# A two-layer hybrid block in float32: the nets' activations made with tokens in rows and turned by DMA and VectorE

## The chip, the core and the metric

The kernel runs on one core of a Trainium2 chip. Its engines work at the same time, each through its own queue: TensorE multiplies (PE in the profile, with its weight loads as PEld), VectorE (DVE) and ScalarE (ACT) do the element-wise work, GpSimd (POOL) a little, and SyncE (SP) issues nearly all transfers. The metric is device time in microseconds (us) of one execution; lower is better. A time is the median of several runs, and the profile is of one execution.

## What is computed

256 tokens of width 1024 pass two layers (DEPTH = 2), each with four steps and a layer norm behind each:

```python
for l in range(DEPTH):
    h = layer_norm(ALPHA * h + 0.5 * swiglu(h, ffn1_gate[l], ffn1_up[l], ffn1_down[l]), ...)
    z = h @ w_in[l]        # split into a short gated convolution, a gated linear recurrence (hgrn2), a pool
    mix = jnp.concatenate([y_conv, y_rec, y_pool], axis=-1) @ w_out[l]
    h = layer_norm(ALPHA * h + mix, ...)
    h = layer_norm(ALPHA * h + cross_attn(h, mem, ca_q[l], ca_k[l], ca_v[l], ca_o[l]), ...)
    h = layer_norm(ALPHA * h + 0.5 * swiglu(h, ffn2_gate[l], ffn2_up[l], ffn2_down[l]), ...)

def swiglu(x, w_gate, w_up, w_down):
    return (jax.nn.silu(x @ w_gate) * (x @ w_up)) @ w_down
```

All of it is float32. The nets' hidden width D_FF is 2816; the attention has 4 heads of 256 over 256 memory tokens. The change touches the nets (`swiglu`, four in all), the first loads of the mixer, and the attention.

## The kernel before

**Precision.** TensorE's fast float32 format (F32R) keeps fewer bits, so every operand is kept as a high and a low part: `split` (lines 60 to 62) has ScalarE cast the high part and VectorE subtract it from the source for the low part. A product is then high x high, high x low and low x high, summed in PSUM. `load` (64 to 91) brings weights by SP in pieces of 1 MB into three buffers `raw`, and splits each piece into two tiles `whi` and two tiles `wlo` of 128 x 1024, of which there are eight each.

**Two forms of a product.** `mm_rows` (127 to 130) has tokens in the output's rows: the activations are the stationary operand, 512 columns of weights stream, three matmuls for each step of 128 in the depth. `mm_cols` (112 to 119) has output features in the rows: the weights are stationary, and the activations' high and low parts stream side by side (512 columns) behind the high weights, and the high part alone (256 columns) behind the low ones, two matmuls for each step; the two sums lie interleaved, and `add` (121 to 124) copies one by ScalarE and adds the other by VectorE. A 512-wide block of features over 256 tokens takes 48 matmuls in the first form and 64 in the second.

**The nets** (`ffn`, 364 to 533) go through the hidden width in chunks of 512, five of them and a last one of 256. For a chunk, gate and up give activations `silu(gate) * up`; `down` then needs them with hidden units in the partitions, as the tiles `ah` and `al` (three pairs). The first chunk (`first`, 374 to 453) is made with tokens in rows, since the weights can be used as they come; its activations are turned by TensorE, eight 128 x 128 transposes into PSUM (`turn`, 391 to 395, line 394), and split from there. The second half of these turnings is put behind the first products of the next chunk (`late`). All other chunks (`hidden`, 455 to 477) are made with hidden units in rows, so nothing is turned. The products with `down` of chunk c - 2's second half and of chunk c - 1's first half follow each chunk (`both`, 493 to 499), into four PSUM banks `dn` that hold the sums over all chunks; the last three slabs make the tail. Other products use four PSUM banks `acc`.

**The joints.** `finish` (284 to 330) adds the residual, takes the norm in steps on VectorE (statistics, then lines 322 and 326 on each half of the row), one token tile after the other. Tile 1's transposes are handed on as `pend` and are run in the middle of the next step's independent products: among the keys (`keys`) ahead of the mixer, among the values (`values`) ahead of the queries, inside the first chunk of a net. The mixer's first matrix (`columns(1280, ...)`) and the queries (`query`) use the normed activations `xT` right after.

**The attention** (815 to 897) makes queries, `weights` (scores and softmax of a head), values, then for each head `turned` (858 to 866: four transposes of the softmax by TensorE, line 862, and a split) and `mixed` (868 to 877: the product with the values). Heads 0 and 1 are turned among the values, heads 2 and 3 after the products of heads 0 and 1.

**What sets the order.** The framework's planner orders each engine's instructions when the program is built, from the order in which they are written, their dependencies and its own costs; each engine then runs its list in order. `tc.issue_after(x)` puts a block's instructions behind x on x's own engine; under `manual_schedule` the written order holds. SP's list holds the transfers: one that waits for its source or its buffer holds up those behind it.

Of the kernel before, what the change touches and what calls it, by code (L numbers as in the profile page):

```python
# [8 lines left out]
F32 = mybir.dt.float32  # L9
# [3 lines left out]
ALU = mybir.AluOpType  # L13
# [33 lines left out]
def model(ctx: ExitStack, tc: tile.TileContext, t: dict, out: bass.AP):  # L47
# [9 lines left out]

    loads = []

# [3 lines left out]

    def load(src, k0, nk, c0, ncol, fine=False):


        hi, lo, todo = [], [], []
        step = 2048 // ncol
        for a in range(k0, k0 + nk, step):
            raw = wp.tile([P, 2048], F32, tag="raw", name="raw", bufs=3)  # L70
            raw = raw.rearrange("p (k c) -> p k c", c=ncol)
            half = step // 2
            part = 1 if fine else step
            for b in range(0, step, part):
                loads.append(nc.sync.dma_start(
                    raw[:, b : b + part, :],
                    src[(a + b) * P : (a + b + part) * P, c0 : c0 + ncol].rearrange("(k p) c -> p k c", p=P),
                ))
# [12 lines left out]
        return Weights(hi, lo, half, todo)  # L91
# [40 lines left out]
    def tok(i):  # L132
        return slice(i * P, (i + 1) * P)
# [150 lines left out]
    def finish(mm, y, scale, gb, last=False, flip=False):  # L284
# [6 lines left out]
        for i in range(NT):  # L291
# [33 lines left out]
            for c in pieces:  # L325
                nc.vector.scalar_tensor_tensor(h[i][:, c], h[i][:, c], rs, b[:, c], op0=ALU.mult, op1=ALU.add)  # L326
# [37 lines left out]
    def ffn(l, name, n, pend=None, last=False, early=None):  # L364
        gate, up, down = (t[f"{name}_{x}"][l] for x in ("gate", "up", "down"))
        with tc.tile_pool(name="ffn", bufs=2, reuse_waits="tile") as fp:
            acts, marks = [], []

            def act_tiles():
                ah = fp.tile([P, 4, SEQ], F32R, tag="ah", name="ah", bufs=3)  # L370
                al = fp.tile([P, 4, SEQ], F32R, tag="al", name="al", bufs=3)
                return ah, al

            def first():

                ah, al = act_tiles()
# [3 lines left out]
                def products(o, w, i, k):  # L380
                    wh, wl = w.at(k, slice(0, CHUNK))
                    mm_rows(o, xTh[:, k, tok(i)], xTl[:, k, tok(i)], wh, wl, k == 0, k == NK - 1)

                def activate(og, ou):
                    s = fp.tile([P, CHUNK], F32, tag="sg", name="sg", bufs=3)
                    v = halves(s)
                    nc.scalar.activation(v, sums(og), AF.Silu)
                    marks.append(nc.vector.tensor_tensor(v, sums(ou), v, op=ALU.mult))
                    return s

                def turn(i, s):
                    pt = acc((P, 4, P))
                    for k in range(4):
                        nc.tensor.transpose(pt[:, k, :], s[:, k * P : (k + 1) * P], idn)  # L394
                    split(ah[:, :, tok(i)], al[:, :, tok(i)], pt)

                if pend is None:
# [34 lines left out]
                    wu = load(up, 0, NK, 0, CHUNK)  # L432
                    ou = [acc((P, CHUNK)) for _ in range(NT)]
                    for a in range(0, NK, 2):
                        for i in range(NT):
                            for k in range(a, a + 2):
                                products(ou[i], wu, i, k)
                    s = [activate(og[i], ou[i]) for i in range(NT)]
                else:
                    s = []  # L440
                    for i in range(NT):
                        og = acc((P, CHUNK))
                        for k in range(NK):
                            products(og, wg, i, k)
                        ou = acc((P, CHUNK))
# [4 lines left out]
                        s.append(activate(og, ou))  # L450
                if pend is not None:
                    turn(0, s[0])
                return (ah, al), lambda: [turn(i, s[i]) for i in range(NT) if i or pend is None]

            def hidden(c0, ncol, late):
                nt = ncol // P
                ah, al = act_tiles()
                w = load(gate, 0, NK, c0, ncol)
                sg = []
                for p in range(nt // 2):  # L460
                    s = fp.tile([P, 2, SEQ], F32, tag="sg", name="sg", bufs=3)
                    for j in range(2):
                        add(s[:, j, :], mm_cols(w, slice((2 * p + j) * P, (2 * p + j + 1) * P), xT))
                    nc.scalar.activation(s, s, AF.Silu)
                    sg.append(s)
                    if late is not None and p == 0:
                        late()
                with tc.issue_after(marks[-1].ins) if late is not None else nullcontext():
                    w = load(up, 0, NK, c0, ncol)
                for p in range(nt // 2):  # L470
                    s = sg[p]
                    r = fp.tile([P, 2, SEQ], F32, tag="up", name="up")
                    for j in range(2):
                        add(r[:, j, :], mm_cols(w, slice((2 * p + j) * P, (2 * p + j + 1) * P), xT))
                    nc.vector.tensor_tensor(s, r, s, op=ALU.mult)
                    split(ah[:, 2 * p : 2 * p + 2, :], al[:, 2 * p : 2 * p + 2, :], s)
                return ah, al

            def slab(c, u):
                w = load(down, c * 4 + 2 * u, 2, 0, DM)  # L480
                ah, al = acts[c]
                return w, ah[:, 2 * u : 2 * u + 2, :], al[:, 2 * u : 2 * u + 2, :]
# [17 lines left out]

            late = None
            for c, (c0, ncol) in enumerate(chunks):
                if c:
                    acts.append(hidden(c0, ncol, late))
                    late = None
                else:
                    a, late = first()
                    acts.append(a)
                    ys = [[acc((P, 512), "dn") for _ in range(2)] for _ in range(NT)]
                if c == 1:  # L510
# [50 lines left out]
    def mixer(l, fill):  # L561
        w_in = t["w_in"][l]
        with tc.tile_pool(name="mix", bufs=1, reuse_waits="tile") as mp:

            def columns(c0, ncol, take, behind=lambda p: None):
                w = load(w_in, 0, NK, c0, ncol)
# [25 lines left out]

            for _ in columns(1280, 512, lambda j, o: add(f[:, :, j, :], o), ev_f):
                pass
# [220 lines left out]
    def attention(l, pend):  # L815
        scale = (DM // HEADS) ** -0.5
        with tc.tile_pool(name="att", bufs=1, reuse_waits="tile") as ap:
# [6 lines left out]
            def query(c, between=None):  # L824
                w = load(t["ca_q"][l], 0, NK, c * CHUNK, CHUNK)
                for p in range(2):
# [31 lines left out]
            def turned(hh):  # L858
                pt = acc()
                for i in range(NT):  # L860
                    for m in range(NT):
                        nc.tensor.transpose(pt[:, m, tok(i)], pr[hh][:, i, tok(m)], idn)
                pTh = ap.tile([P, NT, SEQ], F32R, tag="pTh", name="pTh", bufs=2)
                pTl = ap.tile([P, NT, SEQ], F32R, tag="pTl", name="pTl", bufs=2)
                split(pTh, pTl, pt)
                return pTh, pTl

            def mixed(hh, pT):
# [69 lines left out]
```

## Time and profile before

| what | value |
|---|---|
| time, median of 3 runs (lowest to highest) | 1111.46 us (1111.36 to 1111.53) |
| the profiled execution's own time | 1111.42 us |
| its span (first to last instruction) | 1109.6 us |
| TensorE busy / its weight loads | 1098.6 / 989.2 us |
| VectorE / ScalarE / GpSimd busy | 819.1 / 605.4 / 62.5 us |
| granted TensorE clock | 0.998 |
| moved by DMA | 218.23 MB, mean 197 GB/s |

Busy time is the sum of an engine's instructions. Matmuls overlap in the profile, each being shown for longer than the distance to the next start: the pace is read from the distance of starts, or from a stretch of the chain divided by its count. In rows such as `start us, us, engine line op out<-in xN [idle <-releaser]` the bracket tells how long the engine was idle before and what released it.

### The profile page before, as it was taken

The numbers are of one execution on the slowest core, as the hardware profiler recorded it, in microseconds if no ns is written. First come the engines' busy times: TensorE is split into PE (matmuls) and PEld (weight loads), VectorE is DVE, ScalarE is ACT, GpSimd is POOL, SyncE is SP. The second block draws the span as 40 slices with busy tenths as digits, with TensorE's granted clock in tenths as the row PEclk, the third lists the DMA queues.
The fourth block names the chain that finished last, engine by engine and source line by source line (L and its number), as shares of the span: only waits on it lengthen the run. The fifth ranks groups of instructions, "written<-read, shape, count | busy, mean of one in ns | idle before, by whom it ended". The sixth has DMA issues, their size and how long they took to land.

```text
span 1109.6 us, 15784 instructions
## 1 busy us (share of the span) xinstructions
PE 1098.6 (99%) x6211; PEld 989.2 (89%) x6211; DVE 819.1 (74%) x1177; ACT 605.4 (55%) x895; POOL 62.5 (6%) x112
## 2 busy tenths in 40 slices
PE   9999999999999999999999999999999999999997
PEld 7999988999889889999889999889998998999896
DVE  6777668898888766566677666598988777666665
ACT  6566454665557365555455555456564654654550
POOL 9500000000000000000000000000000000000000
PEclk9999999999999999999999999999999999999999
DMA  8956655744475365665467555655535645656541
GB/s 318 299 185 228 227 199 176 244 142 152 167 268 172 106 236 202 216 228 192 150 229 256 199 192 186 228 190 190 173 133 203 213 154 181 234 190 215 178 177 38
DMA packets 99114, 218.23 MB, mean 197 GB/s; under 512 B 4256, under 2 KB 16832, under 8 KB 99040
## 3 DMA queue, kind: packets, MB, share of 16 engines
q1 hardware_dynamic: 97248, 214.84, 56.4%
q0 software_dynamic: 1216, 1.20, 0.4%
q10 hardware_dynamic: 576, 1.18, 0.3%
q8 instruction: 49, 0.80, 0.3%
q14 instruction: 25, 0.20, 0.1%
HBM read 216.15 MB, written 1.05 MB: 196 GB/s over the span
## 4 chain that ended last, share of the span: by engine, by line
PE 93%; DVE 5%; issue 1%; DMA 0%; ACT 0%; DVEq 0%
PE acc L103 61%; PE dn L103 28%; DVE wlo L62 2%; PE dn L687 1%; PE acc L167 1%; DVE h L326 1%; DVE xT L62 0%; DVE h L312 0%; DVE h L322 0%; PE dn L741 0%; PE dn L664 0%; DMA h<-in_x_dram 0%; PE acc L394 0%; DVE st L314 0%; DVE pTl L62 0%
## 5 line engine op out<-in xcount | busy, mean ns | idle before, releaser
L62 DVE TENSOR_TENSOR wlo<-raw,whi 128x1024 fp32r<-128x1024 f32 (+1 forms) x396 | 470.3, 1211 | 101.2 <-ACT whi L61 66.7
L61 ACT CAST whi<-raw 128x1024 fp32r<-128x1024 f32 (+1 forms) x396 | 398.1, 1041 | 170.8 <-PE dn L103 126.8
L103 PE MATMUL acc<-xT,whi 128*128 128x512 f32 x1600 | 388.3, 381 | 0.7 <-DVE xT L62 0.7
L103 PEld LDWEIGHTS acc<-xT,whi 128*128 128x128 f32 x1600 | 288.9, 190 | 33.8 <-DVE xT L62 1.1
L103 PEld LDWEIGHTS acc<-xT,wlo 128*128 128x128 f32 x1600 | 209.7, 191 | 10.7
L103 PE MATMUL acc<-xT,wlo 128*128 128x256 f32 x1600 | 210.8, 275 | 0.0
L103 PE MATMUL dn<-whi,ah 128*128 128x512 f32 x346 | 131.5, 380 | 0.0
L103 PE MATMUL dn<-wlo,ah 128*128 128x512 f32 x346 | 131.1, 379 | 0.0
L103 PE MATMUL dn<-whi,al 128*128 128x512 f32 x346 | 131.1, 379 | 0.0
L103 PE MATMUL acc<-whi,xT 128*128 128x512 f32 x288 | 88.4, 381 | 0.0
L103 PE MATMUL dn<-whi,xT 128*128 128x512 f32 x288 | 88.3, 382 | 0.1
L124 DVE TENSOR_TENSOR sg<-acc,sg 128x256 f32<-128x256 f32 x72 | 30.4, 422 | 67.4 <-ACT sg L123 67.3
L103 PEld LDWEIGHTS dn<-whi,al 128*128 128x128 f32 x346 | 65.4, 189 | 9.3
L103 PEld LDWEIGHTS dn<-wlo,ah 128*128 128x128 f32 x346 | 65.4, 189 | 9.2
L103 PEld LDWEIGHTS dn<-whi,ah 128*128 128x128 f32 x346 | 65.5, 189 | 8.7
L123 ACT COPY sg<-acc 128x256 f32<-128x256 f32 x72 | 26.7, 371 | 77.9 <-PE acc L103 77.9
L319 POOL TENSOR_TENSOR rs<-rs,nhalf 128x1 f32<-128x1 f32 x16 | 15.0, 934 | 873.7 <-DVE rs L318 873.7
L103 PEld LDWEIGHTS dn<-whi,xT 128*128 128x128 f32 x288 | 54.2, 189 | 7.9 <-ACT whi L61 0.5
L103 PEld LDWEIGHTS acc<-whi,xT 128*128 128x128 f32 x288 | 54.3, 189 | 7.6
L103 PE MATMUL dn<-wlo,xT 128*128 128x512 f32 x144 | 54.8, 380 | 0.3 <-DVE wlo L62 0.3
L103 PE MATMUL acc<-wlo,xT 128*128 128x512 f32 x144 | 54.6, 379 | 0.0
L123 ACT COPY up<-acc 128x256 f32<-128x256 f32 x72 | 26.6, 371 | 46.4 <-PE acc L103 45.3
(196 smaller groups left out, 1070.9 us busy)
## 6 DMA issues: line engine op xcount, KB each, us to landing
raw<-in_ffn_up_dram SPq DMA_DIRECT2D x44, 1024.0 KB, 5.0
raw<-in_ffn_down_dram SPq DMA_DIRECT2D x44, 1024.0 KB, 4.9
raw<-in_ffn_gate_dram SPq DMA_DIRECT2D x42, 1024.0 KB, 5.0
raw<-in_w_in_dram SPq DMA_DIRECT2D x24, 1024.0 KB, 5.0
raw<-in_ca_k_dram SPq DMA_DIRECT2D x8, 1024.0 KB, 4.9
raw<-in_w_out_dram SPq DMA_DIRECT2D x8, 1024.0 KB, 4.9
raw<-in_ca_v_dram SPq DMA_DIRECT2D x8, 1024.0 KB, 5.7
raw<-in_ca_q_dram SPq DMA_DIRECT2D x8, 1024.0 KB, 4.9
```

The source lines that it names most:

```text
L61: nc.scalar.copy(hi, src)
L62: nc.vector.tensor_tensor(lo, src, hi.bitcast(F32), op=ALU.subtract)
L103: nc.tensor.matmul(o, w, x, start=start, stop=stop)
L123: nc.scalar.copy(dst, o[:, 1])
L124: nc.vector.tensor_tensor(dst, o[:, 0], dst, op=ALU.add)
L167: nc.tensor.transpose(pt[:, k, :], src[:, (4 * j + k) * P : (4 * j + k + 1) * P], unit)
L319: nc.gpsimd.tensor_tensor(rs, rs, nhalf[:, 0:1], op=ALU.pow)
L326: nc.vector.scalar_tensor_tensor(h[i][:, c], h[i][:, c], rs, b[:, c], op0=ALU.mult, op1=ALU.add)
L687: nc.tensor.matmul(o[:, hh], kc[:, hh, :], view(qf, hh * P + c, (other - c, 2), (2 * c, a), (1, c)), start=True, stop=True,)
```

## The change

1. Chunks 1 to 4 of each net are made with tokens in rows too (`all_products`, `activate`, `gated`), gate and up each by k in pairs for both token tiles. The last chunk of 256 keeps the other form (`last_hidden`).
2. All activations made so, the first chunk's too, are turned without TensorE (`turn`): four DMAs deal the tokens of tile `s` over groups of 32 partitions (token 4q + b of a tile to partition q of a group, slot b), 512 bytes a piece, and VectorE transposes 32 x 32 blocks, one instruction for each token tile, with strided patterns on both sides. Hidden unit 4p + k of a chunk then lies in partition p, slot k; so these chunks' rows of `down` are loaded in that order (`strewn`), 8 KB in one piece per partition.
3. Low parts of the weights for the mixer's first matrix and for both halves of the queries are put behind the last step of the norm on VectorE (`issue_after(normed[-1].ins)`).
4. In the attention heads 2 and 3 are turned among the values as well, through `dn` banks, into the places of the queries of heads 0 and 1, which have been used by then.

```diff
-    loads = []
+    loads, normed = [], []
...
                 loads.append(nc.sync.dma_start(
                     raw[:, b : b + part, :],
-                    src[(a + b) * P : (a + b + part) * P, c0 : c0 + ncol].rearrange("(k p) c -> p k c", p=P),
+                    src[:, c0 : c0 + ncol].rearrange("(p k) c -> p k c", p=P)[:, a + b : a + b + part, :]
+                    if strewn
+                    else src[(a + b) * P : (a + b + part) * P, c0 : c0 + ncol].rearrange("(k p) c -> p k c", p=P),
                 ))
...
-                nc.vector.scalar_tensor_tensor(h[i][:, c], h[i][:, c], rs, b[:, c], op0=ALU.mult, op1=ALU.add)
+                normed.append(nc.vector.scalar_tensor_tensor(
+                    h[i][:, c], h[i][:, c], rs, b[:, c], op0=ALU.mult, op1=ALU.add
+                ))
...
+            def all_products(w):
+                o = [acc((P, CHUNK)) for _ in range(NT)]
+                for a in range(0, NK, 2):
+                    for i in range(NT):
+                        for k in range(a, a + 2):
+                            products(o[i], w, i, k)
+                return o
+
+            def activations():
+                return fp.tile([P, NT, CHUNK], F32, tag="sg", name="sg", bufs=1)
+
+            def activate(s, i, og):
+                nc.scalar.activation(halves(s[:, i, :]), sums(og), AF.Silu)
+
+            def gated(s, i, ou):
+                v = halves(s[:, i, :])
+                nc.vector.tensor_tensor(v, sums(ou), v, op=ALU.mult)
...
+            def turn(s):
+                ah, al = act_tiles()
+                x = fp.tile([P, 4, NT, P], F32, tag="dealt", name="dealt", bufs=1)
+                for a in range(4):
+                    nc.sync.dma_start(x[a * 32 : a * 32 + 32], s[:, :, a * P : (a + 1) * P])
+                for i in range(NT):
+                    d = fp.tile([P, 4, P], F32, tag="up", name="square")
+                    nc.vector.transpose(
+                        d.rearrange("p k (i b) -> p b k i", b=4), x[:, :, i, :].rearrange("p b (j k) -> p b k j", k=4)
+                    )
+                    split(ah[:, :, tok(i)], al[:, :, tok(i)], d)
+                return ah, al
...
-                def turn(i, s):
-                    pt = acc((P, 4, P))
-                    for k in range(4):
-                        nc.tensor.transpose(pt[:, k, :], s[:, k * P : (k + 1) * P], idn)
-                    split(ah[:, :, tok(i)], al[:, :, tok(i)], pt)
...
-            def hidden(c0, ncol, late):
...
+            def hidden(c0):
+                s = activations()
+                o = all_products(load(gate, 0, NK, c0, CHUNK))
+                for i in range(NT):
+                    activate(s, i, o[i])
+                o = all_products(load(up, 0, NK, c0, CHUNK))
+                for i in range(NT):
+                    gated(s, i, o[i])
+                return turn(s)
...
             def slab(c, u):
-                w = load(down, c * 4 + 2 * u, 2, 0, DM)
+                if c < len(chunks) - 1:
+                    w = load(down[c * CHUNK : (c + 1) * CHUNK], 2 * u, 2, 0, DM, strewn=True)
+                else:
+                    w = load(down, c * 4, 2, 0, DM)
...
-            for _ in columns(1280, 512, lambda j, o: add(f[:, :, j, :], o), ev_f):
+            for _ in columns(1280, 512, lambda j, o: add(f[:, :, j, :], o), ev_f, normed[-1].ins):
...
             def query(c, between=None):
-                w = load(t["ca_q"][l], 0, NK, c * CHUNK, CHUNK)
+
+                with tc.issue_after(normed[-1].ins):
+                    w = load(t["ca_q"][l], 0, NK, c * CHUNK, CHUNK)
...
             def turned(hh):
-                pt = acc()
+                pt = acc(tag="dn" if hh > 1 else "acc")
...
-                pTh = ap.tile([P, NT, SEQ], F32R, tag="pTh", name="pTh", bufs=2)
-                pTl = ap.tile([P, NT, SEQ], F32R, tag="pTl", name="pTl", bufs=2)
+                if hh < 2:
+                    pTh = ap.tile([P, NT, SEQ], F32R, tag="pTh", name="pTh", bufs=2)
+                    pTl = ap.tile([P, NT, SEQ], F32R, tag="pTl", name="pTl", bufs=2)
+                else:
+
+                    pTh, pTl = (x[:, 2 * hh - 4 : 2 * hh - 2, :] for x in (qTh, qTl))
...
-                {2: lambda: (weights(2), weights(3)), 6: lambda: pT.extend((turned(0), turned(1)))},
+                {
+                    2: lambda: (weights(2), weights(3)),
+                    6: lambda: pT.extend((turned(0), turned(1))),
+                    7: lambda: pT.extend((turned(2), turned(3))),
+                },
             )
             for hh in range(HEADS):
                 mixed(hh, pT[hh])
-                if hh + 2 < HEADS:
-                    pT.append(turned(hh + 2))
```

More of the change, by code (lines that the diff above doesn't have):

```diff
@@ L62, in split, with load @@
         nc.vector.tensor_tensor(lo, src, hi.bitcast(F32), op=ALU.subtract)
-    def load(src, k0, nk, c0, ncol, fine=False):
+    def load(src, k0, nk, c0, ncol, fine=False, strewn=False):
         hi, lo, todo = [], [], []
@@ L366, in ffn @@
         with tc.tile_pool(name="ffn", bufs=2, reuse_waits="tile") as fp:
-            acts, marks = [], []
+            acts = []
             def act_tiles():
@@ L372, in act_tiles, with products @@
                 return ah, al
+            def products(o, w, i, k):
+                wh, wl = w.at(k, slice(0, CHUNK))
+                mm_rows(o, xTh[:, k, tok(i)], xTl[:, k, tok(i)], wh, wl, k == 0, k == NK - 1)
+            def all_products(w):
[5 more added lines that the diff above has]
+                return o
@@ L374, in first @@
             def first():
-                ah, al = act_tiles()
+                s = activations()
                 wg = load(gate, 0, NK, 0, CHUNK, fine=pend is None)
                 wu = load(up, 0, NK, 0, CHUNK) if pend is not None else None
[L380 to L389, printed above, removed]
@@ L432, in first @@
                     wu = load(up, 0, NK, 0, CHUNK)
[L433 to L438, printed above, removed]
+                    ou = all_products(wu)
+                    for i in range(NT):
+                        activate(s, i, og[i])
+                        gated(s, i, ou[i])
                 else:
-                    s = []
                     for i in range(NT):
@@ L444, in first @@
                             products(og, wg, i, k)
+                        activate(s, i, og)
                         ou = acc((P, CHUNK))
@@ L449, in first @@
                             products(ou, wu, i, k)
[L450 to L453, printed above, removed]
-            def hidden(c0, ncol, late):
-                nt = ncol // P
+                        gated(s, i, ou)
+                return turn(s)
+            def hidden(c0):
+                s = activations()
+                o = all_products(load(gate, 0, NK, c0, CHUNK))
+                for i in range(NT):
+                    activate(s, i, o[i])
+                o = all_products(load(up, 0, NK, c0, CHUNK))
+                for i in range(NT):
+                    gated(s, i, o[i])
+                return turn(s)
@@ L457, in hidden, with last_hidden @@
+            def last_hidden(c0):
                 ah, al = act_tiles()
[L458 to L461, printed above, removed]
+                s = activations()[:, 0, :].rearrange("p (j c) -> p j c", j=2)
+                r = fp.tile([P, 2, SEQ], F32, tag="up", name="up")
+                for m, o in ((gate, s), (up, r)):
+                    w = load(m, 0, NK, c0, 2 * P)
@@ L462, in hidden @@
                     for j in range(2):
[L463 to L476, printed above, removed]
+                        add(o[:, j, :], mm_cols(w, slice(j * P, (j + 1) * P), xT))
@@ L477, in hidden @@
+                    if m is gate:
+                        nc.scalar.activation(s, s, AF.Silu)
+                nc.vector.tensor_tensor(s, r, s, op=ALU.mult)
+                split(ah[:, 0:2, :], al[:, 0:2, :], s)
                 return ah, al
             def slab(c, u):
-                w = load(down, c * 4 + 2 * u, 2, 0, DM)
+                if c < len(chunks) - 1:
+                    w = load(down[c * CHUNK : (c + 1) * CHUNK], 2 * u, 2, 0, DM, strewn=True)
+                else:
+                    w = load(down, c * 4, 2, 0, DM)
@@ L499, in both @@
                             rows_of(a, i, k, m, c == u == k == 0, apart)
-            late = None
             for c, (c0, ncol) in enumerate(chunks):
-                if c:
-                    acts.append(hidden(c0, ncol, late))
-                    late = None
-                else:
-                    a, late = first()
-                    acts.append(a)
-                    ys = [[acc((P, 512), "dn") for _ in range(2)] for _ in range(NT)]
+                if not c:
+                    acts.append(first())
+                    ys = [[acc((P, 512), "dn") for _ in range(2)] for _ in range(NT)]
+                else:
+                    acts.append(hidden(c0) if ncol == CHUNK else last_hidden(c0))
                 if c == 1:
@@ L563, in mixer, with columns @@
         with tc.tile_pool(name="mix", bufs=1, reuse_waits="tile") as mp:
-            def columns(c0, ncol, take, behind=lambda p: None):
-                w = load(w_in, 0, NK, c0, ncol)
+            def columns(c0, ncol, take, behind=lambda p: None, after=None):
+                with tc.issue_after(after) if after is not None else nullcontext():
+                    w = load(w_in, 0, NK, c0, ncol)
                 for j in range(ncol // P):
```

## The prediction, made before the changed kernel ran

> **What bounds the kernel now.** I read the page first: its span, the busy shares, and the engines' shares of the chain that ended last.
>
> ```profile
> span 1109.6 us, 15784 instructions
> ```
>
> ```profile
> PE 1098.6 (99%) x6211; PEld 989.2 (89%) x6211; DVE 819.1 (74%) x1177; ACT 605.4 (55%) x895; POOL 62.5 (6%) x112
> ```
>
> ```profile
> PE 93%; DVE 5%; issue 1%; DMA 0%; ACT 0%; DVEq 0%
> ```
>
> TensorE is busy 99% of the span and is 93% of the chain; VectorE has a quarter of the span to spare. So time falls by what leaves TensorE's queue and by the pauses in it, and by little else. The profiled execution took 1111.42 us, 1.82 of it outside the span; the median of the three runs is 1111.46, so I make the sum against 1111.42 and carry it over as it is.
>
> Next the chain in order of time (start, length, what). Its unbroken stretches give TensorE's pace:
>
> ```profile
> 18.94 15.60 PE acc L103 x80
> 34.54 0.87 PE acc L394 x8
> ...
> 429.25 20.96 PE acc L103 x128
> 450.21 10.36 PE dn L103 x48
> 460.57 20.96 PE acc L103 x128
> ...
> 740.90 0.61 DVE xT L62
> ```
>
> The 128 at 429.25 are gate and up of one 512-wide chunk in the old form: 64 a matrix, half of them 512 wide and half 256, 10.48 us. The 48 at 450.21 are all 512 wide: 10.36 us, 0.216 each; the 256-wide ones are then (10.48 - 32 x 0.216) / 32 = 0.112. The last line is VectorE's low part of xT: the chain leaves TensorE there, which means a pause. TensorE's timeline shows the pauses of one layer: at the mixer's start,
>
> ```profile
> 193.44 0.38 PE L103 MATMUL acc<-mT,whi 128*128 128x512 f32 x1
> 193.99 1.75 PE L103 MATMUL acc<-xT,whi 128*128 128x512 f32 x7 [0.17 <-DVE xT L62]
> ```
>
> at the queries' start, after a row of eight undisturbed turnings for comparison,
>
> ```profile
> 34.38 1.04 PE L394 MATMUL acc<-idn,sg 128*128 128x128 f32 x8
> ...
> 310.46 1.22 PE L167 MATMUL acc<-idn,h 128*128 128x128 f32 x8
> ...
> 313.89 0.38 PE L103 MATMUL acc<-whi,mT 128*128 128x512 f32 x1
> 314.43 1.78 PE L103 MATMUL acc<-xT,whi 128*128 128x512 f32 x7 [0.16 <-DVE xT L62]
> ```
>
> and at the heads' turning:
>
> ```profile
> 355.20 0.60 PE L862 MATMUL acc<-idn,e 128*128 128x128 f32 x4
> 355.95 0.35 PE L103 MATMUL acc<-pTh,vh 128*128 128x256 f32 x1
> ```
>
> Starts that should lie 0.216 apart are 0.55 apart before 193.99 (0.33 lost) and 0.54 before 314.43 (0.32 lost). Eight turnings take 1.22 in place of 1.04 (0.18 lost). Four turnings of a head should fill 4 x 0.109 (0.87 / 8), but 0.75 pass before 355.95 (0.31 lost). That is 1.14 a layer; with the second layer alike, which the line at 740.90 bears out for the mixer, 2.28.
>
> **Part 1, tokens in rows.** In chunks 1 to 4 of four nets, 32 matrices go from 64 matmuls to 48, with the same columns streamed. First chunks are made so already, and into acc: the 15.60 for 80 at 18.94 is 48 such (10.36) and half a matrix of the old form (5.24), so the pace holds there. Gain 32 x (10.48 - 10.36) = 3.84 us, all on the path. The Trainium skill ("TensorE: Matmul & The Clock Gate", Back-to-back issue gap) states a gap of N/2.4 + 2.5 ns for one matmul by itself. That is 215.8 for 512, with which the trace agrees, and 109.2 for 256, where the trace has 112; by it the gain would be 1.28. The rows decide: 3.84.
>
> **Part 2, low parts behind norms.** VectorE's timeline at the mixer's start:
>
> ```profile
> 183.64 1.22 DVE L62 TENSOR_TENSOR wlo<-raw,whi 128x1024 fp32r<-128x1024 f32 x1
> 184.78 0.69 DVE L314 BATCH_NORM_STATS2 st<-h 128x6 f32<-128x512 f32 x1
> 185.38 1.21 DVE L62 TENSOR_TENSOR wlo<-raw,whi 128x1024 fp32r<-128x1024 f32 x1
> ...
> 188.30 1.41 DVE L326 SCALAR_TENSOR_TENSOR h<-h,rs,lnb 128x512 f32<-128x512 f32 x2
> ...
> 193.16 1.29 DVE L62 TENSOR_TENSOR xT<-acc,xT 128x512 fp32r<-128x512 f32 x2
> ```
>
> Two low parts of the mixer's first matrix stand ahead of the norm's last step (L326). Moved behind it, they let the norm end 2.43 us sooner, at 187.3, and there is room for them before xT's own low parts come ready; the loads themselves are not moved, only VectorE's step on them. What is late next is the fourth low part. If xT's came no sooner, the moved 2.43 would end at 194.45 + 2.43 = 196.9; TensorE, ready at 193.66, wants the first low part after seven high products, at 195.2, and the fourth 6 x 0.112 later, at 195.8: 1.1 lost in place of 0.33. Bounds for the four joints (two mixers, two queries): from 2 x (0.33 + 0.32 + 0.18) = 1.66 gained to 4 x 1.1 - 1.66 = 2.7 lost. I take 1.66 gained, since VectorE does the same work and what is wanted first now comes first.
>
> **Part 3, heads' turning.** The turnings of heads 2 and 3 move ahead of all heads' products, into dn banks. Bounds: 0.62 gained (0.31 a layer), or as much lost if VectorE, with two more low parts to make before the products, is late with the first. I take 0.31 gained, half.
>
> **Part 4, the nets' turning leaves TensorE.** The 32 turnings of first chunks (L394) go, four times 0.87: 3.49 us gained (TensorE has nothing to do in their place). Instead each of 20 chunks gets a deal of 512 KB in four issues and two transposes by VectorE. The rows for VectorE, min/median/max in ns, then the only transposes of before (mean ns after the comma):
>
> ```profile
> L124 DVE TENSOR_TENSOR sg<-acc,sg x72: 416/424/426, 33.4 to 1076.7; 128x256 f32<-128x256 f32 x72
> L475 DVE TENSOR_TENSOR sg<-up,sg x36: 647/691/693, 48.4 to 1082.4; 128x512 f32<-128x512 f32 x36
> L62 DVE TENSOR_TENSOR al<-sg,ah x36: 676/689/694, 49.8 to 1084.1; 128x512 fp32r<-128x512 f32 x36
> L388 DVE TENSOR_TENSOR sg<-acc,sg x8: 691/692/692, 28.0 to 949.9; 128x512 f32<-128x512 f32 x8
> ```
>
> ```profile
> L192 DVE STREAM_TRANSPOSE turned<-m 128x512 f32<-128x512 f32 x4 | 2.8, 702 | 0.0
> ```
>
> A chunk from 1 to 4 loses eight adds (424) and two products (691), 4.77 us, and gains two gated products (692) and two transposes (702, or twice that if the strided pattern costs), 2.8 to 4.2. A first chunk gains 1.4 to 2.8. With 26% of VectorE's span free, neither is worth anything in time: TensorE's products cover them.
>
> The deal stands in SP's queue, in order with the weights' loads. The rows for that: two loads of gate, the cast that follows a load, issue sizes with median time to landing, and what SP waits for (total, times, longest):
>
> ```profile
> 431.75 9.95 SPq L75 DMA_DIRECT2D raw<-in_ffn_gate_dram  x2
> ```
>
> ```profile
> L61 ACT CAST whi<-raw 128x1024 fp32r<-128x1024 f32 (+1 forms) x396 | 398.1, 1041 | 170.8 <-PE dn L103 126.8
> ```
>
> ```profile
> raw<-in_ffn_gate_dram SPq DMA_DIRECT2D x42, 1024.0 KB, 5.0
> ...
> m<-in_mem_dram POOLq DMA_DIRECT2D x32, 32.0 KB, 6.1
> ```
>
> ```profile
> SPq L75 <- DVE wlo L62: 518.2, 119, 13.1
> ```
>
> The four issues wait for the gated product, and loads queued behind them wait too. The cover: the second of the two loads is issued by 441.70 and lands 5.0 later, at 446.70; two casts (1.04) and a low part (1.22) make it 450.0, and TensorE wants that matrix at 460.57. A hold of up to 10.6 us costs nothing; beyond that each chunk pays the excess. Against long holds: SP is mostly waiting for one of three raw buffers (518.2 us in 119 waits), so it cannot stand further ahead than three loads. The deal itself: from 2.5 us (half of a 1024 KB load's 5.0, for half the bytes) to 24.4 (four in series at the 6.1 of the mem loads, whose pieces are 128 bytes); its pieces are 512 bytes and its four issues need not wait for each other, so I take 5. From the end of up: two products 1.4, the deal 5, then a transpose, a cast and a low part, 2 to 3 more, under 10 in all. A first chunk's square is wanted 20.96 after (the whole next chunk), the others at least 5 later still. Nothing is late.
>
> **Sum.** 1111.42 - 3.84 - 1.66 - 0.31 - 3.49 = 1102.1 us.
>
> **Rivals.** (a) The joints do not gain: the waits only change names, or low parts come late. For it: VectorE has hardly an idle moment in the rows of part 2. With parts 2 and 3 at nothing 1104.1; with part 2's loss, up to 1106.8. (b) Rows gain less: new stretches of 48 run at 10.44, a third of the gain, as if the 256-wide ones cost next to nothing extra: 1104.7. Against: 10.48 and 10.36 stand in the chain. The page cited in part 1 would have it so. (c) Slower: the dealt squares come late. With 24.4 us for a deal, a first chunk's is ready 1.4 + 24.4 + 2 = 27.8 after up, 6.8 late; four such are 27 us: 1129. It costs from a deal of 17.6 us on and makes the kernel slower from some 20 (four times 2.3 is the whole gain of 9.3); against it stands the 5.0 of twice the bytes. (d) No change: holds in SP's queue of 11 us eat 0.45 in each of 20 chunks: 1111. (e) The change does not do what it says, the planner putting loads or products elsewhere in passing: between 1104 and 1111.
>
> **How the numbers follow.** Forecast 0.60, (a) 0.22, (b) 0.04, (c) 0.06, (d) 0.03, (e) 0.05. 0.2% is 2.2 us, about what a measurement of this kernel can tell from no change. Faster is the forecast, (a), (b) and most of (e), 0.90; same 0.04; slower 0.06. The range runs from 1100.9 (all of 2.28, and 0.9 more from pauses not listed here) to 1106.3, (a) with most of its loss; it holds the forecast, (b) and nearly all of (a), some 0.85.
>
> **What would show it.** Right: TensorE has 544 instructions fewer (512 products, 32 turnings); a chunk's gate and up are 96 acc products in 20.72 in the chain; L394 is gone; two STREAM_TRANSPOSE a chunk, under 1.4 us each; nothing of TensorE waits for al or ah. At the joints the low parts follow L326, and the first product on xT starts 0.22 after the one before. Wrong: TensorE waits for wlo at the joints (part 2), for ah or al (c), or for whi while SP waits for the gated product (d); or the new acc stretches run above 0.216 (b).

## The result and the profile after

The changed kernel took 1102.32 us (median of five runs, 1101.39 to 1102.94) against 1111.46 (1111.36 to 1111.53): a ratio of 0.9916, interval 0.9905 to 0.9928. Run again unaltered beside other runs of the kernel before it took 1101.37 (four runs, 1101.36 to 1101.42) against 1111.55, a ratio of 0.9906 (0.9893 to 0.9920). The wider scatter of the first set did not come back, so later comparisons with "the changed kernel" use 1101.37; the kernel before took 1111.41 to 1111.55 beside every later set of runs.

Traces are compared on the profiled execution: 1101.39 us, where before had 1111.42, so 10.03 less. First its span, the busy shares and the engines' shares of the chain:

```profile
span 1099.7 us, 14684 instructions
...
PE 1089.5 (99%) x5667; PEld 968.6 (88%) x5667; DVE 834.5 (76%) x1089; ACT 566.2 (51%) x767; POOL 63.9 (6%) x112
...
PE 98%; DVE 1%; issue 0%; DMA 0%; ACT 0%; DVEq 0%
```

TensorE has 6211 - 5667 = 544 instructions fewer, 512 products and 32 turnings. VectorE fell from 5% of the chain to 1%: the chain no longer leaves TensorE at the joints. (That share is not time that TensorE stood: 4% of the span is 44 us, and its pauses at the joints were 0.33 us and less. A chain that leaves an engine does not by itself mean that the engine paused, as the prediction has it; the timeline tells the pauses.) Yet VectorE's own work did not shrink; it grew by 15.4 us (834.5 against 819.1).

Now the changed kernel's chain of waits in order of time (start, length, what):

```profile
19.08 31.08 PE acc L106 x144
...
425.04 20.72 PE acc L106 x96
445.76 10.36 PE dn L106 x48
```

The 144 are the first net's first up and both matrices of its second chunk, 48 each, in one run; the 96 are gate and up of a chunk, where 128 in 20.96 stood before. All go at 0.216.

The joints, in TensorE's timeline: first the mixer, then the queries, then the heads.

```profile
191.74 0.38 PE L106 MATMUL acc<-mT,whi 128*128 128x512 f32 x1
191.96 1.67 PE L106 MATMUL acc<-xT,whi 128*128 128x512 f32 x7
...
308.36 1.04 PE L170 MATMUL acc<-idn,h 128*128 128x128 f32 x8
...
311.61 0.38 PE L106 MATMUL acc<-whi,mT 128*128 128x512 f32 x1
311.82 1.67 PE L106 MATMUL acc<-xT,whi 128*128 128x512 f32 x7
...
348.08 1.04 PE L888 MATMUL dn<-idn,e 128*128 128x128 f32 x8
...
350.04 0.38 PE L106 MATMUL acc<-whi,mT 128*128 128x512 f32 x1
350.25 0.27 PE L106 MATMUL acc<-pTh,vh 128*128 128x256 f32 x1
```

The first product on xT starts 0.22 and 0.21 after its neighbour, no bracket names a wait, and eight turnings take 1.04 again. The turnings of heads 2 and 3 stand as one undisturbed eight, and the heads' first product follows its neighbour by 0.21. VectorE's timeline at the mixer has the order that part 2 meant:

```profile
184.44 1.41 DVE L329 SCALAR_TENSOR_TENSOR h<-h,rs,lnb 128x512 f32<-128x512 f32 x2
...
186.10 1.21 DVE L62 TENSOR_TENSOR wlo<-raw,whi 128x1024 fp32r<-128x1024 f32 x1
...
190.77 1.28 DVE L62 TENSOR_TENSOR xT<-acc,xT 128x512 fp32r<-128x512 f32 x2
```

The norm's last step (line 329 here) starts at 184.44 in place of 188.30. TensorE is 1.70 earlier at this place (191.74 against 193.44), so the norm is 2.2 sooner and xT's low parts are 0.7 sooner, which is more than the 0.33 that was lost. The pauses of TensorE that are left (0.40 at 268.65 and at 811.23, 0.23 at three nets' turnings) were there before.

Last the new work, from the views of the two tiles (instructions with min/median/max in ns), and the longest holds of SP's queue (total, times, longest):

```profile
L411 DVE STREAM_TRANSPOSE square<-dealt x40: 1578/1651/1765, 42.4 to 1059.5; 128x512 f32<-128x512 f32 x40
```

```profile
L408 SPq DMA_DIRECT2D dealt<-sg x80: 608/617/1617, 31.5 to 1053.5; - x80
...
DMA to landing us min/median/max: 2.8/3.3/9.0
```

```profile
SPq L76 <- DVE wlo L62: 667.0, 151, 13.1
SPq L408 <- DVE sg L399: 48.2, 18, 3.3
```

A transpose takes 1.65 us, above the 1.40 that I had as the worse end. The holds of SP's queue for the gated product are at most 3.3 us, well under the 10.6 that cost nothing. But one of the 80 issues took 9.0 us to land, and the first net's first chunk shows what that leaves, in the timelines of SP, VectorE and TensorE:

```profile
31.45 2.75 SPq L408 DMA_DIRECT2D dealt<-sg  x4
```

```profile
42.36 3.13 DVE L411 STREAM_TRANSPOSE square<-dealt 128x512 f32<-128x512 f32 x2
45.28 0.72 DVE L62 TENSOR_TENSOR al<-square,ah 128x512 fp32r<-128x512 f32 x1
46.17 0.69 DVE L62 TENSOR_TENSOR al<-square,ah 128x512 fp32r<-128x512 f32 x1 [0.17 <-ACT ah L61]
```

```profile
50.00 0.38 PE L106 MATMUL dn<-whi,ah 128*128 128x512 f32 x1
```

From the first issue to the last low part pass 46.86 - 31.45 = 15.4 us, and TensorE's first product on them starts at 50.00. No wait, then, but a room of 3 us between the last low part and the first product, where the prediction reckoned with 11.

### The profile page after: what moved, and what is told of

The parts are those of the page before. It is cut to its first block, busy times and chain, and to the rows that moved or that the text cites. A ratio compares the mean times of both kernels' runs of the same rounds, so it can differ in the third digit from the quotient of the medians.

```text
span 1099.7 us, 14684 instructions
## 1 busy us (share of the span) xinstructions
PE 1089.5 (99%) x5667; PEld 968.6 (88%) x5667; DVE 834.5 (76%) x1089; ACT 566.2 (51%) x767; POOL 63.9 (6%) x112
## 3 DMA queue, kind: packets, MB, share of 16 engines
HBM read 216.15 MB, written 1.05 MB: 198 GB/s over the span
## 4 chain that ended last, share of the span: by engine, by line
PE 98%; DVE 1%; issue 0%; DMA 0%; ACT 0%; DVEq 0%
PE acc L106 64%; PE dn L106 30%; PE acc L170 1%; PE dn L711 1%; DMA h<-in_x_dram 0%; PE dn L765 0%; PE dn L688 0%; DVE wlo L62 0%; PE dn L754 0%; PE dn L764 0%; PE dn L888 0%; PE acc L888 0%; DVE yr L772 0%; DVE h L329 0%; DVE h L325 0%
## 5 line engine op out<-in xcount | busy, mean ns | idle before, releaser
L106 PE MATMUL acc<-whi,xT 128*128 128x512 f32 x1312 | 394.9, 379 | 0.0
L106 PEld LDWEIGHTS acc<-whi,xT 128*128 128x128 f32 x1312 | 247.8, 189 | 35.0
L106 PE MATMUL acc<-wlo,xT 128*128 128x512 f32 x656 | 248.6, 379 | 0.0
L106 PE MATMUL acc<-xT,whi 128*128 128x512 f32 x576 | 141.9, 382 | 0.0
L106 PEld LDWEIGHTS acc<-wlo,xT 128*128 128x128 f32 x656 | 124.0, 189 | 17.5
L106 PEld LDWEIGHTS acc<-xT,whi 128*128 128x128 f32 x576 | 104.2, 190 | 11.2
L106 PEld LDWEIGHTS acc<-xT,wlo 128*128 128x128 f32 x576 | 75.5, 191 | 3.9
L106 PE MATMUL acc<-xT,wlo 128*128 128x256 f32 x576 | 75.9, 275 | 0.0
L411 DVE STREAM_TRANSPOSE square<-dealt 128x512 f32<-128x512 f32 x40 | 63.4, 1656 | 0.5 <-DMA dealt<-sg 0.5
L315 DVE SCALAR_TENSOR_TENSOR h<-h,dn 128x512 f32<-128x512 f32 x31 | 21.2, 684 | 33.9 <-PE dn L106 33.9
```

Source lines behind the costliest of these rows:

```text
L106: nc.tensor.matmul(o, w, x, start=start, stop=stop)
L315: nc.vector.scalar_tensor_tensor(v, v, ALPHA / scale, sums(y[i][n]), op0=ALU.mult, op1=ALU.add)
L411: nc.vector.transpose(d.rearrange("p k (i b) -> p b k i", b=4), x[:, :, i, :].rearrange("p b (j k) -> p b k j", k=4))
```

## The experiments

My theory was the sum of the prediction: rows 3.84, joints 1.66, the heads, 3.49 of turnings, and a deal that is hidden. Rivals were that the joints give nothing, that rows gain only a third, and that the deal's cover is nearly used up.

**The joints alone** (the kernel before with the prediction's part 2 only).

```diff
-                w = load(t["ca_q"][l], 0, NK, c * CHUNK, CHUNK)
+                with tc.issue_after(normed[-1].ins):
+                    w = load(t["ca_q"][l], 0, NK, c * CHUNK, CHUNK)
...
-            for _ in columns(1280, 512, lambda j, o: add(f[:, :, j, :], o), ev_f):
+            for _ in columns(1280, 512, lambda j, o: add(f[:, :, j, :], o), ev_f, normed[-1].ins):
```

> The kernel before with nothing but the low parts of the mixer's first matrix and of the queries put behind the norm. Theory (part 2 of the prediction): the four waits close, 1111.46 - 1.66 = 1109.8, and the pauses before the first products on xT are gone from TensorE's timeline. Rival (a): the waits only change names, 1111.4, with TensorE waiting on wlo at the same places. For the spread of the changed kernel: if the closed joints bring it, it shows here, above 1 us; if the deals do, the spread stays at 0.2 to 0.4.

Measured: 1109.49 (eleven runs) against 1111.55, ratio 0.9979 (0.9970 to 0.9988): 2.06 less, with an interval of about 1 us on either side. TensorE's timeline at the mixer and at the queries:

```profile
193.38 0.38 PE L103 MATMUL acc<-mT,whi 128*128 128x512 f32 x1
193.59 1.67 PE L103 MATMUL acc<-xT,whi 128*128 128x512 f32 x7
...
313.23 0.38 PE L103 MATMUL acc<-whi,mT 128*128 128x512 f32 x1
313.45 1.67 PE L103 MATMUL acc<-xT,whi 128*128 128x512 f32 x7
```

The same starts lie 0.21 and 0.22 apart, with nothing else changed. The rival that the joints give nothing is refuted. The trace accounts for the 1.66 and for 0.36 more: before, the start behind each of the four pauses was late too, by 0.08 at the mixers and 0.10 at the queries (the seven products took 1.75 and 1.78 there, and 1.67 here). That is 2.02.

**The heads alone** (the kernel before with the prediction's part 3 only; its diff is the change's lines on `turned`, from `acc(tag=...)` on).

> The kernel before with nothing but heads 2 and 3 turned among the values. Theory: the two pauses of 0.31 close, 1111.46 - 0.62 = 1110.8. Prediction: half of it, 1111.15. Rival: VectorE is late with the first heads' low parts in place of it, 1111.5 to 1112.1.

Measured: 1110.76 (eleven runs), ratio 0.9991 (0.9982 to 1.0000), 0.79 less. The runs hardly tell that from nothing; the trace has no pause left at the heads' first products (353.15 comes 0.21 after its neighbour), and all 0.62 of it is gone.

**Rows undone, whole** (the changed kernel with chunks 1 to 4 in columns; they share the one activation buffer).

```diff
             def hidden(c0):
-                s = activations()
-                o = all_products(load(gate, 0, NK, c0, CHUNK))
...
+                ah, al = act_tiles()
+                w = load(gate, 0, NK, c0, CHUNK)
+                both_halves = activations()
...
+                    s = both_halves[:, p, :].rearrange("p (j c) -> p j c", j=2)
```

> The changed kernel with gate and up of chunks 1 to 4 made with hidden units in rows again (no deal, no transposes there; first chunks stay dealt, norms and heads as changed). Theory: 32 x 0.12 = 3.84 us come back, 1102.3 + 3.84 = 1106.2, and the chain shows 128 products in 20.96 in place of 96 in 20.72. Rival (b): 1.28 come back, 1103.6. If the 16 deals of these chunks cost time anywhere, less than 3.84 comes back; if deals bring the spread, it shrinks here to under 0.6.

Measured: 1130.19, ratio 1.0165 (1.0152 to 1.0179), 28.8 above the changed kernel: not what any theory said, and not the price of columns. ScalarE's and TensorE's timelines tell why:

```profile
42.25 1.20 ACT L126 COPY sg<-acc 128x256 f32<-128x256 f32 x4 [1.28 <-DMA dealt<-sg]
```

```profile
44.16 0.79 PE L106 MATMUL dn<-whi,ah 128*128 128x512 f32 x1 [4.20 <-ACT ah L61]
```

The second chunk's sums go into the buffer that the first chunk's deal still reads. With all four acc banks full, TensorE stands 4.20 us; its next instruction is a product on the first chunk's square, which comes behind the same deal (the bracket's ah), and VectorE's add that frees the first bank starts at 44.35. What follows is in the windows of that stretch (per engine busy us and count for PE, PEld, DVE, ACT, POOL, then the granted clock, the share of the DMA engines and GB/s):

```profile
40.00:44.00 4.00, 0.00 (x0) 0.00 (x0) 3.94 (x4) 2.69 (x7) 2.97 (x6) 0.94 1.08 264
44.00:46.00 2.00, 1.84 (x4) 1.46 (x5) 2.00 (x5) 0.73 (x2) 1.22 (x3) 0.50 1.07 323
46.00:50.00 4.00, 4.00 (x15) 3.52 (x14) 2.14 (x4) 2.10 (x3) 3.32 (x6) 0.50 1.06 313
...
422.40:425.80 3.40, 3.40 (x11) 2.81 (x11) 2.93 (x6) 1.56 (x4) 0.00 (x0) 0.50 0.51 199
```

After the pause TensorE worked on at a granted clock of 0.50 until 50.00, some 6 us, which costs 3 more; from 50.00 to 56.00 the clock was 0.97. Each of the four nets has such a pause, by starts 4.36 once and 3.49 three times, 14.8 in all. The stretch at 0.50 is as long in the third net and 3.4 us in the second (the last row) and the fourth; in the four stretches TensorE lost 10.1 by its starts. The chain has 128 products in 20.96 again, so the columns' own price is 3.84, and 14.8 + 10.1 + 3.84 is 28.7 of the 28.8. The rows' part is there as predicted, under a late deal that costs more than six times as much.

**Rows undone in chunks 2 to 4** (the second chunk stays in rows, so that no sums wait for the first chunk's deal).

```diff
-                    acts.append(hidden(c0) if ncol == CHUNK else last_hidden(c0))
+                    acts.append((hidden if c < 2 else hidden_columns if ncol == CHUNK else last_hidden)(c0))
```

> The changed kernel with gate and up of chunks 2, 3 and 4 made with hidden units in rows again; chunks 0 and 1 stay as changed, so that no add waits for a first chunk's deal. Theory (part 1): 24 x 0.12 = 2.88 us come back, 1101.4 to 1102.3 plus 2.88 = 1104.3 to 1105.2, with 128 products in 20.96 in those chunks and no pause of TensorE. Rival (b): 24 x 0.04 = 0.96, 1102.3 to 1103.3.

Measured: 1106.95 (1104.80 to 1109.15), ratio 0.9958 (0.9946 to 0.9971), 5.6 above the changed kernel. The chain has the pace again, and TensorE's timeline one new pause:

```profile
428.20 20.96 PE acc L106 x128
449.16 10.36 PE dn L106 x48
```

```profile
67.98 1.78 PE L106 MATMUL acc<-xT,whi 128*128 128x512 f32 x7 [1.86 <-DVE sg L127]
```

Each chunk in columns costs 20.96 - 20.72 = 0.24: 2.88 for twelve. The pause (2.03 between starts) is the second chunk's deal in the first net, which took 10 us to land, while the third chunk's sums, now in columns, wait for its buffer; with it the sum comes to 4.9 of the 5.6. The last 0.7 and the scatter of the runs I did not resolve.

**First chunks turned by TensorE again** (rows everywhere; the four first chunks' squares in the middle of the next gate), and beside it **all twenty chunks** so.

```diff
+                    if late is not None and a == 4:
+                        late()
...
+            def squares(s, ah, al):
+                for i in range(NT):
+                    pt = acc((P, 4, P))
+                    for k in range(4):
+                        nc.tensor.transpose(pt[:, k, :], s[:, i, k * P : (k + 1) * P], idn)
+                    split(ah[:, :, tok(i)], al[:, :, tok(i)], pt)
```

> The changed kernel, but the first chunk of each net is turned by TensorE again (in the middle of the next chunk's gate) and its down weights loaded in the old order; chunks 1 to 4 stay dealt. Theory (part 4): 4 x 0.87 = 3.49 us come back, 1101.4 to 1102.3 plus 3.49 = 1104.9 to 1105.8. Rival: the first chunks' deals cost something themselves (they have the least room), and less comes back, 1103 or below.

> The changed kernel with tokens in rows in all 512-wide chunks, but all 20 of them turned by TensorE: no deal, no transposes on VectorE. Theory: 20 x 0.87 = 17.4 us come back, 1118.8 to 1119.7, so rows pay only because the turning left TensorE. If TensorE's turning costs more than its own time (a pause for a bank or for the splits), above 1121. If the deals and transposes cost the changed kernel time that the profile does not show, less than 17.4 comes back.

Measured: 1106.33, ratio 0.9959 (0.9946 to 0.9971), and 1131.22, ratio 1.0181 (1.0167 to 1.0195): 5.0 and 29.8 above the changed kernel. Both are above the theory's 3.49 and 17.4, and each trace shows a pause that the edit brought in the first net, of TensorE for VectorE:

```profile
41.62 0.48 PE L106 MATMUL acc<-whi,xT 128*128 128x512 f32 x1 [0.69 <-DVE al L62]
```

```profile
43.25 1.11 PE L410 MATMUL acc<-idn,sg 128*128 128x128 f32 x4 [8.73 <-DVE sg L401]
```

By starts the first is 0.86; the second, with another one right after it, 9.8. With them the sums are 4.4 of 5.0 and 27.2 of 29.8; behind the second pause the clock was 0.50 until 49.5, which cost TensorE 2.7 more and makes it 29.9. The long pause is the new order's, not the price of turning: VectorE had stood 11.55 us for a load of the memory tokens (until 37.31), which the planner had put ahead of the gated product. What is left is close to 0.87 a chunk, so TensorE's turning was dearer than the deal, which cost nothing that these two runs show. Here the Trainium skill ("VectorE: DVE Perf Modes", Rules for kernel authors) advises TensorE for a 128 x 128 transpose wherever PSUM will do as its destination; with TensorE 99% busy that advice lost in this kernel.

**The cover doubled** (each chunk dealt twice, the second deal after the first, and transposed twice), then **transposes alone doubled**.

```diff
-                for a in range(4):
-                    nc.sync.dma_start(x[a * 32 : a * 32 + 32], s[:, :, a * P : (a + 1) * P])
+                for _ in range(2):
+                    for a in range(4):
+                        nc.sync.dma_start(x[a * 32 : a * 32 + 32], s[:, :, a * P : (a + 1) * P])
```

> The changed kernel with each deal done twice, the second into the same tile behind the first, and each of VectorE's transposes done twice: 10.5 MB more of transfers and some 66 us more of VectorE (834 to 900 us of 1100). Theory: both lie under TensorE's products, within 0.3 us of the changed kernel, 1101.4 to 1102.6. Rival (c), squares late: where the doubled deal passes its room of 17.6 us in a first chunk, TensorE pauses on ah there and its time rises by 2 us a chunk or more, 1105 to 1115.

> The changed kernel with VectorE's transposes done twice and the deals once: 66 us more of VectorE. The squares of first chunks then come 3.3 us later, against a room of 3.1, 4.5, 4.9 and 3.6 us in the profile after. Theory: covered but for some tenths in the first net, 1101.4 to 1103.0. Rival: VectorE is too late with other low parts, and TensorE pauses in all chunks, 1105 or more. With the run that doubled both it tells which of the two used up the room.

Measured: 1114.78 (1114.13 to 1117.60), ratio 1.0038 (1.0025 to 1.0050), 13.4 above the changed kernel; and 1101.42 (1101.37 to 1101.56), ratio 0.9908 (0.9893 to 0.9923), no difference. SP's and TensorE's timelines with two deals:

```profile
31.59 12.56 SPq L409 DMA_DIRECT2D dealt<-sg  x8
44.21 1.26 SPq L76 DMA_DIRECT2D raw<-in_ffn_gate_dram  x2
```

```profile
52.44 0.48 PE L106 MATMUL dn<-whi,ah 128*128 128x512 f32 x1 [2.09 <-ACT ah L61]
```

Two things went wrong at once. The squares came late (52.44): ScalarE, which waits for the same buffer, went on at 48.24 in place of 42.02, so the deals landed 6 us later, and the first low part, behind doubled transposes, came 7.9 later (53.88 against 46.00); by starts TensorE lost 3.0 there. And two loads of gate that followed the deal at 34.30 in the changed kernel were issued at 44.21; the same happened in later chunks (11.04 us of deals from 82.51 on), and TensorE paused for low parts and weights, 2.09 us before 76.74 and 3.57 before 105.89. By starts TensorE lost 5.4 on squares in the four nets, 6.8 on weights in the first, and 3.1 behind 105.89, where the clock was 0.50 until 113.7: 15.3 of the 16.1 by which this trace's span is longer. (The profiled execution, 1117.60, is the slowest of the five.) VectorE's timeline with the transposes doubled:

```profile
43.09 6.07 DVE L412 STREAM_TRANSPOSE square<-dealt 128x512 f32<-128x512 f32 x4
49.02 0.66 DVE L62 TENSOR_TENSOR al<-square,ah 128x512 fp32r<-128x512 f32 x1
```

The first token tile's low part came at 49.68 and the second's at 50.54, both 3.7 later than in the changed kernel, and TensorE waited for neither. So the room is larger than the 3 us from the last low part to the first product: the second tile's parts are wanted only behind the first tile's twelve products, 2.6 us later. VectorE's 55 us more (889.7 busy against 834.5) cost nothing; what passed the room when both were doubled is the deal (it was not doubled alone).

**Nets behind their norms** (low parts of gate and up of a net's first chunk put behind the norm as well), and **half of up only**.

```diff
+                with tc.issue_after(normed[-1].ins) if pend is not None else nullcontext():
+                    wg = load(gate, 0, NK, 0, CHUNK, fine=pend is None)
+                    wu = load(up, 0, NK, 0, CHUNK) if pend is not None else None
```

```diff
+                    wu = load(up, 0, NK // 2, 0, CHUNK)
+                    with tc.issue_after(normed[-1].ins):
+                        late = load(up, NK // 2, NK // 2, 0, CHUNK)
```

> The changed kernel with the same order for the nets that follow a norm: the low parts of the first chunk's gate and up are put behind the norm's last step. In the profile after, eight turnings still take 1.05 in place of 0.87 at three places (385.14, 558.13 and 927.72), where they wait for the norm. Theory: these three pauses of 0.2 close, 0.5 to 0.7 us less than the changed kernel. Rival: up's and gate's low parts come too late instead, TensorE waits on wlo after them, 0 to 3 us more.

> The changed kernel with the low parts of only the second half of up's first matrix put behind the norm in the three nets that follow one; gate and up's first half, whose products run while the norm is made, stay ahead. Theory: the norm ends one low part (1.2 us) sooner and the three pauses of 0.23 at the turnings close, 0.5 to 0.7 us less than the changed kernel. Rival: the planner uses the freed place otherwise, no difference or a new pause on wlo.

Measured: 1119.91, ratio 1.0080 (1.0067 to 1.0092), 18.5 above the changed kernel; and 1101.10 (1100.93 to 1101.35), ratio 0.9906 (0.9892 to 0.9919), 0.27 below it. TensorE's timeline of the first and its windows:

```profile
381.29 1.94 PE L170 MATMUL acc<-idn,h 128*128 128x128 f32 x8 [3.58 <-DVE h L329]
```

```profile
381.00:385.00 4.00, 3.71 (x14) 3.28 (x15) 4.00 (x5) 2.30 (x3) 0.00 (x0) 0.58 0.70 259
385.00:387.00 2.00, 2.00 (x11) 1.73 (x11) 2.00 (x3) 0.15 (x1) 0.00 (x0) 1.00 0.79 204
```

Gate's products of the first token tile are the work that covers the norm of the second, and they need the very low parts that were put behind it: 3.74 lost between starts, three times. Behind these pauses the clock was 0.50 for 3.4, 6.8 and 3.4 us (the first is the 0.58 in the window's mean), and TensorE lost 1.6, 3.0 and 2.0 more. Together that is 17.8 of the 18.5. With only the late half of up moved, the chain of waits has the nets' turnings undisturbed:

```profile
385.23 0.87 PE acc L170 x8
386.11 1.95 PE acc L106 x9
```

In the changed kernel these eight take 1.05. Three pauses of 0.23 are gone in the trace (span 1099.2 against 1099.7); the runs cannot tell 0.3 from nothing. It has the lowest median of the versions that I ran.

**The transpose's patterns** (chunk by chunk: both sides strided, only the result, only the source, neither; hidden units and tokens then land elsewhere in the squares, so only the time counts).

```diff
-                        d.rearrange("p k (i b) -> p b k i", b=4), x[:, :, i, :].rearrange("p b (j k) -> p b k j", k=4)
+                        d.rearrange("p k (i b) -> p b k i", b=4) if n in (0, 1)
+                        else d.rearrange("p k (b i) -> p b k i", b=4),
+                        x[:, :, i, :].rearrange("p b (j k) -> p b k j", k=4) if n in (0, 2)
+                        else x[:, :, i, :].rearrange("p b (k j) -> p b k j", k=4),
```

> One look at VectorE's transposes in four patterns, one a chunk, turn by turn: strided in and out (as changed), dense in, dense out, both dense. The dense ones put hidden units or tokens in other places than the down weights expect; only their time is of interest. In the changed kernel the 40 take 1.58 to 1.77 us, where the only dense ones of before took 0.70. If the strides cost, the dense ones take 0.70 and the mixed ones lie between; if the neighbours' traffic costs (eight of these took 1.04 to 1.17 while TensorE paused), all take 1.6.

Measured: 1101.73, one execution. VectorE's timeline, two transposes a row; in order the result strided, the source strided, neither, both:

```profile
66.27 2.93 DVE L412 STREAM_TRANSPOSE square<-dealt 128x512 f32<-128x512 f32 x2
85.76 2.98 DVE L412 STREAM_TRANSPOSE square<-dealt 128x512 f32<-128x512 f32 x2 [1.80 <-DMA dealt<-sg]
114.96 1.30 DVE L412 STREAM_TRANSPOSE square<-dealt 128x512 f32<-128x512 f32 x2
145.99 3.20 DVE L412 STREAM_TRANSPOSE square<-dealt 128x512 f32<-128x512 f32 x2
```

One strided side costs nearly as much as two, 1.5 us each against 1.6; only dense on both sides gives 0.65. The strides are not all of it. In the run with rows undone whole, all eight transposes, strided on both sides, fell into TensorE's pauses, the second of each pair at the pause's end:

```profile
L411 DVE STREAM_TRANSPOSE square<-dealt x8: 1081/1126/1166, 42.3 to 977.3; 128x512 f32<-128x512 f32 x8
```

They took 1.08 to 1.17 us; in the changed kernel, beside a working TensorE, they take 1.58 to 1.77. So some 0.45 of a strided transpose is the strides' and 0.5 more comes with its neighbours' work; which neighbour's was not tested.

## Why the prediction was right, and where its steps were not

**The sum.** It gave 9.3 against the profiled execution and the trace shows 10.03. Its terms as measured are 3.84 + 1.66 + 0.62 + 3.49 = 9.61. The last 0.4 is a term that the prediction left out: the start behind each pause was late as well, by 0.36 at the joints (the experiment with the joints alone) and 0.14 at the heads. Less the 0.14 by which the first long stretch starts later (19.08 against 18.94), that makes 9.97. That the first median, 1102.32, lay 0.2 from the forecast was luck; the repeat, 1101.37, and the profiled execution lie 0.7 below it.

**Part 1, right.** 96 in 20.72 in every such chunk of the chain, and 0.24 a chunk back when chunks 2 to 4 are undone. The rival that rows gain a third falls: the formula of the Trainium skill that is quoted there would have the 256-wide products cost next to nothing extra, and the stretches of 20.72 and 20.96 say otherwise.

**Part 2, right in mechanism and size.** The low parts that stood ahead of the norm were the cause: with part 2 alone the starts close up. What I had named as late next, the fourth low part, did not stop TensorE. The two runs on the nets' norms draw the limit of the step: a low part moved behind the norm gains only if no product that covers the norm needs it.

**Part 3, mis-sized.** I took half of 0.62; all of it went, without the wait for a low part that I had set against it.

**Part 4, right in its gain, wrong in its cover.** TensorE lost 3.49 of turnings and waits for no square. But three numbers behind "nothing is late" failed. The transposes take 1.65, not 0.70 to 1.40: the strides bring them to some 1.1, and beside a working TensorE they take 1.6. So VectorE's work grew by 15.4, where the prediction's rows give between 26 less and 2 more. The first net's first deal took 10.5 us (31.45 to 41.9; ScalarE, which waits for it, goes on at 42.02), not 5. The 5 held, at 5.1 to 5.8, for fifteen of the twenty deals; the first chunks' took 8.7 to 10.5 and the second chunk's in the first net 9.8. These had more loads of weights in flight beside them, which as the cause is not tested apart. And the whole way was 15.4 us in that first chunk and 11 to 12 in the quick ones, not under 10. The forecast held because 18.6 were there: most of the room that was meant as spare was used. The doubled cover bears out rival (c), that a late deal costs, and rival (d), that loads held behind it cost too. Rival (c) had the cost begin at a deal of 17.6 us; a first deal of 16.3 us (31.59 to 47.85), with the transposes doubled behind it, already cost 3.0.

## What to carry to other kernels

Where TensorE is busy 99% of the span, price each edit in its instructions and in single pauses: the turning that goes through DMA and VectorE was free here because it landed in time. State the room as a time (here low parts that came 3.7 us later cost nothing, and 7.9 later cost 3.0), from the first chunk, where deals took longest, and not from a median landing time. A step put behind a norm must not feed the products that hide that norm.

## What the runs showed of the hardware that I had not expected

- A pause of TensorE cost twice from some length on. After idle times of 3.3 to 8.7 us the granted clock was 0.50 for several us, as in the windows above, in stretches of 3.4 or 6.8 us (10.2 with the 8.7 us pause itself), and TensorE lost 1.6 to 3.1 us more. After 0.69, 1.86 and 2.09 it stayed at 1.00; no run has a pause between 2.1 and 3.3. The Trainium skill ("TensorE: Matmul & The Clock Gate", Part 1: The HAM clock gate) gives about 3.4 us of idle window for it, on a window that does not start with the pause; the traces agree, the shortest such pauses being 3.3 by their brackets.
- A 128 x 512 transpose by VectorE of 32 x 32 blocks took 0.65 to 0.70 us dense and 1.5 to 1.8 with a stride of four words on one side or on both, beside a working TensorE; strided on both, while TensorE stood, 1.08 to 1.17.
- A deal of 512 KB in four issues took 5.1 to 5.8 us from the first issue to landing in fifteen chunks and 8.7 to 10.5 in the other five, though the median of a single issue is 3.3.
